# A two-layer transformer block on one core: norm steps ahead of weight splits in the order of work, and an output projection that ends tile by tile

## The chip, the cores and the metric

One core of a Trainium2 chip runs the whole program. The metric is the time of one execution on the device in microseconds (us); the kernel before takes 1361.4 us (median of three runs, 1358.92 to 1363.43). The engines are TensorE (PE, with its weight loads PEld), VectorE (DVE), ScalarE (ACT), GpSimd (POOL) and SyncE (SP), which here only issues DMAs. Each engine carries out its own instructions in their order; engines wait for one another by semaphores.

## What is computed

Two layers act on 256 rows of `ctx` and 256 rows of `x`, each row 1024 wide, all in fp32. Cut to what matters:

```python
for l in range(2):
    with_ctx = l == 0
    sx1, ax1, gx1, sx2, ax2, gx2 = split(silu(c) @ w_ada[l] + b_ada[l], 6)      # likewise for ctx
    hx = rmsnorm(x, g_pre_mix[l]) * (1.0 + ax1) + sx1                           # likewise hc from ctx
    yc, yx = token_mixer(hc, hx, w_in[l], ..., w_out[l])                        # mLSTM, HGRN2, attention, then @ w_out
    x = x + gx1 * rmsnorm(yx, g_post_mix[l])                                    # "post-norm"
    hx = rmsnorm(x, g_pre_ffn[l]) * (1.0 + ax2) + sx2                           # "norm"
    x = x + gx2 * rmsnorm((silu(hx @ w_gate[l]) * (hx @ w_up[l])) @ w_down[l], g_post_ffn[l])
    # with_ctx: the same two updates for ctx
return x
```

## The kernel before

The 512 rows lie in four tiles of 128: tiles 0 and 1 are `ctx` (half 0), tiles 2 and 3 are `x` (half 1). The residual of a tile is `R[t]`. In layer 0 both halves go through everything, half 1 first in the FFN; in layer 1 only half 1 goes on after the mixer.

**Weights.** Each fp32 product is made of reduced-precision products of a high and a low part. `wload` (L279) brings a piece of a weight matrix (512 KB or less) into `wraw` by a DMA on SP (L292; three buffers), rounds it into `whi` on ACT (L295) and forms the rest `wlo` on DVE (L296), with two buffers of each. Activations lie likewise as `hT[0]` (high) and `hT[1]` (low), transposed. Every piece gives matmuls of `hT[0]` and `hT[1]` with `whi`, and of `hT[0]` with `wlo`, all at L300.

**Modulation sums.** `silu(c) @ w_ada` is not made on PE: `ada_group` loads `araw` pieces of 512 KB on SP (L210; two buffers) and DVE adds each, scaled, to `accq` and `acc` (L224, L226). It is a generator that is stepped between other work, for the next layer in particular.

**Norms.** `post_norm` (L443) sums the squares in `zss` on DVE (L446), takes the power on POOL (L448) and updates `R[t]` on DVE (L450); then the norm takes the square of `R[t]` on ACT (L411), `rstd` on POOL (L401, L402) and scales into `nsc` on DVE (L413). `norm_T` transposes `nsc` on PE in four banks of PSUM `pt` (L430), applies the modulation on ACT (L436) and DVE (L438), rounds `hT[0]` on ACT (L440) and forms `hT[1]` on DVE (L441).

**The output projection.** `out_first` does the half of `w_out` that is known early, `out_rest` the other half: four column blocks `cb`, each two PSUM halves of a bank, for both tiles of a half. When two blocks are done, `ev_z` takes the result out: `Z` on DVE (L1151) and its squares on ACT (L1153). After the FFN's down projection `ev_d` does the like in quarters (L1274, L1277, L1278). `late_norm` is the norm of half 1 at the start of layer 1, built when that layer's first matmuls are written.

**What sets the order.** The program is written as straight code, and a scheduler puts each engine's instructions in an order by priority: the place in the code, less an offset where the code asks for one. `wload`'s two splits have an offset of 2000 (`AHEAD`); norms, sums and projections have none. Where two instructions are ready, the one with the smaller number goes first on its engine; the order is fixed when the program is built. Tiles from a pool are handed out in the order of the code, so a step also waits for the tile that it reuses.

## Time and profile before

| | us |
|---|---|
| median of three runs | 1361.4 (1358.92 to 1363.43) |
| the profiled execution | 1362.55 |
| its span, first to last instruction | 1360.8 |
| PE busy | 1294.5 (95% of the span) |
| DVE busy | 897.5 (66%) |
| ACT busy | 619.0 (45%) |
| POOL busy | 198.9 (15%) |
| mean granted clock of PE, share of full | 0.984 |

In the page, busy time is a share of the whole span, and the chain of work that ended last is followed back from the last instruction to what released each step. A timeline gives for each instruction its start, its length, its engine and line, what it writes and reads, a count where several follow on one another, and in brackets how long the engine was idle before it and what ended that. A table of stretches gives for each stretch its length, the busy time and instructions (x) of PE, PEld, DVE, ACT and POOL, then PEclk, the busy share of the DMA engines and the GB/s moved. PEclk is the clock that PE was granted as a share of full: 0.50 is 1.2 GHz, 1.00 is 2.4 GHz.

### The profile page before, as it was taken

What the parts mean: (1) busy time and instruction counts of PE and PEld (TensorE: products, weight loads), DVE (VectorE), ACT (ScalarE), POOL (GpSimd) and SP (SyncE); (2) the same over time, 40 slices, a digit from 0 to 9 for tenths busy, and PEclk for the clock granted to TensorE, in tenths of its full rate; (3) what the DMA queues carried; (4) which work ended last, traced back from release to release, by engine and by line L of the source; (5) the groups of instructions that cost most, each with busy time, mean ns of one, the idle gap of its engine ahead of it and who ended that gap; (6) DMA issues with size and microseconds to landing.
All of it is one profiled execution on the core that took longest, in us unless ns stands there. A gap on an engine that the chain in (4) does not pass through costs nothing.

```text
span 1360.8 us, 25400 instructions
## 1 busy us (share of the span) xinstructions
PE 1294.5 (95%) x10166; PEld 1159.7 (85%) x10166; DVE 897.5 (66%) x1586; ACT 619.0 (45%) x1176; POOL 198.9 (15%) x316
## 2 busy tenths in 40 slices
PE   7998999999989999999999999899999997999997
PEld 5776889788988898998899888778897997999997
DVE  4899989564688997476335348566856555555555
ACT  3436452586255652222322236546526825544443
POOL 3123102111042200001000013133111201000001
PEclk9999999999989899999999999899999999899999
DMA  9872526132244687487335335532331314456663
GB/s 284 239 217 65 174 62 194 36 114 70 94 140 156 196 257 219 140 258 245 96 94 186 93 108 141 142 93 65 101 95 50 121 47 139 124 181 181 184 184 125
DMA packets 171348, 194.20 MB, mean 143 GB/s; under 512 B 10620, under 2 KB 158502, under 8 KB 171230
## 3 DMA queue, kind: packets, MB, share of 16 engines
q1 hardware_dynamic: 169806, 188.89, 45.9%
q0 software_dynamic: 1424, 3.68, 0.9%
q8 instruction: 80, 1.31, 0.4%
q14 instruction: 38, 0.31, 0.1%
HBM read 191.47 MB, written 1.08 MB: 141 GB/s over the span
## 4 chain that ended last, share of the span: by engine, by line
PE 79%; DVE 8%; ACT 5%; POOL 3%; issue 2%; DMA 2%; SPq 0%; DVEq 0%; POOLq 0%; ACTq 0%
PE mm L300 65%; PE mx L1102 2%; DVE wlo L296 2%; PE mx L957 1%; PE mx L979 1%; ACT whi L295 1%; PE mm L1090 1%; POOL rstd L402 1%; PE mx L430 1%; PE mx L973 1%; ACT Dt L1011 1%; DMA wraw<-in_w_ffn_down_dram 1%; PE mx L855 1%; PE ada L231 1%; POOL rstd L401 1%
## 5 line engine op out<-in xcount | busy, mean ns | idle before, releaser
L295 ACT CAST whi<-wraw 128x1024 fp32r<-128x1024 f32 (+1 forms) x254 | 259.0, 1021 | 447.0 <-PE mm L300 388.1
L296 DVE TENSOR_TENSOR wlo<-wraw,whi 128x1024 fp32r<-128x1024 f32 (+1 forms) x250 | 299.5, 1199 | 199.5 <-ACT whi L295 97.0
L300 PE MATMUL mm<-hT,whi 128*128 128x256 f32 (+1 forms) x1920 | 356.9, 337 | 3.6 <-ACT hT L440 2.1
L300 PEld LDWEIGHTS mm<-hT,whi 128*128 128x128 f32 x1920 | 296.9, 192 | 42.5 <-issue 3.3
L300 PE MATMUL mm<-whi,hT 128*128 128x256 f32 (+1 forms) x1792 | 265.7, 294 | 4.5 <-ACT hT L1133 2.2
L300 PEld LDWEIGHTS mm<-whi,hT 128*128 128x128 f32 x1792 | 234.5, 193 | 22.3 <-issue 10.5
L300 PE MATMUL mm<-hT,wlo 128*128 128x256 f32 (+1 forms) x960 | 185.5, 335 | 0.0
L300 PEld LDWEIGHTS mm<-hT,wlo 128*128 128x128 f32 x960 | 150.4, 191 | 17.5 <-issue 0.4
L300 PE MATMUL mm<-wlo,hT 128*128 128x256 f32 (+1 forms) x896 | 138.8, 292 | 0.0
L300 PE MATMUL mm<-whi,GT 128*128 128x256 f32 x1032 | 134.6, 284 | 1.0 <-ACT whi L295 1.0
L300 PEld LDWEIGHTS mm<-whi,GT 128*128 128x128 f32 x1032 | 128.2, 192 | 3.7 <-issue 1.7
L300 PEld LDWEIGHTS mm<-wlo,hT 128*128 128x128 f32 x896 | 119.1, 192 | 8.4 <-issue 7.6
L226 DVE SCALAR_TENSOR_TENSOR accq<-araw,csil,accq 128x1024 f32<-128x1024 f32 x63 | 81.3, 1295 | 25.9 <-DMA araw<-in_w_ada_dram 25.5
L300 PE MATMUL mm<-wlo,GT 128*128 128x256 f32 x516 | 71.3, 283 | 0.7 <-DVE wlo L296 0.7
L300 PEld LDWEIGHTS mm<-wlo,GT 128*128 128x128 f32 x516 | 65.9, 192 | 1.3 <-DVE wlo L296 1.3
L226 DVE SCALAR_TENSOR_TENSOR acc<-araw,csil,acc 128x1024 f32<-128x1024 f32 x49 | 63.7, 1321 | 4.5 <-DMA araw<-in_w_ada_dram 4.4
L401 POOL TENSOR_SCALAR rstd<-hss 128x1 f32<-128x1 f32 (+2 forms) x44 | 17.0, 386 | 242.7 <-ACT hsq L631 159.0
L1278 POOL TENSOR_TENSOR Z<-Z,gg 128x256 f32<-128x256 f32 x18 | 15.8, 889 | 246.7 <-ACT sqz L1277 246.7
L1254 DVE TENSOR_TENSOR sg<-sg,mm 128x256 f32<-128x256 f32 (+1 forms) x48 | 24.7, 518 | 34.2 <-PE mm L300 33.5
L964 ACT ACTIVATE e<-mx,damx 128x512 f32<-128x512 f32 (+1 forms) x48 | 29.3, 617 | 24.9 <-DVE damx L961 24.9
L786 ACT COPY Ck<-Kh 128x512 f32<-128x512 f32 (+1 forms) x56 | 28.8, 524 | 25.7 <-DVE Kh L811 17.9
L957 PE MATMUL mx<-qkT,qkT 48*128 48x512 f32 (+1 forms) x96 | 34.2, 562 | 6.3 <-ACT e L964 5.5
(275 smaller groups left out, 1474.2 us busy)
## 6 DMA issues: line engine op xcount, KB each, us to landing
araw<-in_w_ada_dram SPq DMA_DIRECT2D x80, 512.0 KB
wraw<-in_w_in_dram SPq DMA_DIRECT2D x68, 512.0 KB
wraw<-in_w_ffn_gate_dram SPq DMA_DIRECT2D x48, 512.0 KB
wraw<-in_w_ffn_up_dram SPq DMA_DIRECT2D x48, 512.0 KB
wraw<-in_w_ffn_down_dram SPq DMA_DIRECT2D x44, 512.0 KB
wraw<-in_w_out_dram SPq DMA_DIRECT2D x24, 512.0 KB
aw<-in_w_ada_dram SPq DMA_DIRECT2D x16, 512.0 KB
wraw<-in_w_in_dram SPq DMA_DIRECT2D x12, 256.0 KB
```

What stands on the lines that cost most here:

```text
L226: V.scalar_tensor_tensor(out=a, in0=raw, scalar=csil[:, k, r:r + 1], in1=a, op0=ALU.mult, op1=ALU.add)
L231: PE.matmul(ps[32 * j:32 * j + 32, :], lhsT=esel[:, r, :], rhs=accs[j // 2][r][:, (j % 2) * 512:(j % 2 + 1) * 512], start=r == 0, stop=r = ...
L295: S.copy(hi[:, :nk, :n], raw[:, :nk, :n])
L296: (eng or V).tensor_tensor(lo[:, :nk, :n], raw[:, :nk, :n], hi[:, :nk, :n], op=ALU.subtract)
L300: PE.matmul(ps, lhsT=lhs, rhs=rhs, start=first, stop=last, skip_group_check=True)
L401: G.tensor_scalar(o[:, :width], ss, 1.0 / n, EPS, ALU.mult, ALU.add)
L786: S.copy(C[:, q0:].rearrange("p (a b i) -> p b a i", b=2, i=m), vap(K_, 2 * m * pq0, [[512 + m, 2], [2 * m, np_], [1, m]]))
L957: PE.matmul(ps[:, :nk], lhsT=qkT[0][64 * j:64 * j + DA_D, h, t * P:(t + 1) * P], rhs=qkT[1][64 * j:64 * j + DA_D, h, :nk], start=True, sto ...
L964: S.activation(e[:, j, :nk], pp[j][:, :nk], AF.Exp, bias=mx[:, 2 + j:3 + j], scale=sc, accum_out=mx[:, 4 + j:5 + j])
L1102: PE.matmul(po[:, i, d_, :], lhsT=W[d_, s_][0][:, t * P - W[d_, s_][2]:(t + 1) * P - W[d_, s_][2]], rhs=Vml[:, s_, h, :], start=n_ == 0, s ...
L1254: V.tensor_mul(sg[:, :n], sg[:, :n], ps)
L1278: (V if cb == 3 else G).tensor_tensor(zs, zs, gg[1 if t < 2 else 0][:, cb * 256:(cb + 1) * 256], op=ALU.mult)
```

## The change

It has three parts. `CHAIN = 4000`: the post-norms and norms before the FFN, after the FFN and at the start of layer 1 get an offset of 4000, more than the weight splits' 2000. The output projection of the last half (half 0 in layer 0, half 1 in layer 1) does column blocks 0 and 1 as before; for blocks 2 and 3 it does all that belongs to one tile, takes `Z` out, and does this tile's post-norm right there, inside the offset; then the other tile. So the post-norm of that half no longer stands in the FFN's part. `NAH = 2`: `norm_T` asks for its first two banks at once and writes the transposes of its first tile into both before those of its second.

```diff
--- before.py
+++ after.py
@@ -78,9 +78,11 @@
 
 NMM = 4
 
-HP1, AHEAD = 20, 2000
+HP1, AHEAD, CHAIN = 20, 2000, 4000
 
 WARM = (7, 0, 10, 0, 2, 4, 6, 3)
+
+NAH = 2
 
 KPOOL = (0, 1, 0, 0, 0, 0, 0)
 
@@ -423,11 +425,20 @@
         xn, hs = scr
         if xs is None:
             xs = [norm_rows(2 * hf + i, xn[:, i]) for i in range(2)]
+        pts = [pst([P, 2, 2, P]) for _ in range(NAH)]
+
+        for i in range(2):
+            for kp in range(NAH):
+                for kk in range(2):
+                    PE.transpose(pts[kp][:, kk, i, :], xs[i][:, (2 * kp + kk) * P:(2 * kp + kk + 1) * P], ident)
         for kp in range(KD // 2):
-            pt = pst([P, 2, 2, P])
-            for kk in range(2):
-                for i in range(2):
-                    PE.transpose(pt[:, kk, i, :], xs[i][:, (2 * kp + kk) * P:(2 * kp + kk + 1) * P], ident)
+            if kp < NAH:
+                pt = pts[kp]
+            else:
+                pt = pst([P, 2, 2, P])
+                for kk in range(2):
+                    for i in range(2):
+                        PE.transpose(pt[:, kk, i, :], xs[i][:, (2 * kp + kk) * P:(2 * kp + kk + 1) * P], ident)
             h = hs[:, kp % 2]
             for kk in range(2):
                 k = 2 * kp + kk
@@ -1171,14 +1182,25 @@
             for t in tt_:
                 Z[t] = yp.tile([P, D], F32, tag=f"Y{t}", name=nm("Z"))
                 zss[t] = sm.tile([P, 2], F32, tag=f"zss{t}", name=nm("zss"))
+            ws = {}
             for cb in range(4):
-                hi, lo = wload([w_out[l, 0:512, cb * 256:(cb + 1) * 256]])
+                hi, lo = ws[cb] = wload([w_out[l, 0:512, cb * 256:(cb + 1) * 256]])
+                if hf != halves[-1] or cb < 2:
+                    for t in tt_:
+                        out_mm(t, cb, hi, 0, True, False, False)
+                    for t in tt_:
+                        out_mm(t, cb, lo, 0, False, False, True)
+                        if cb % 2:
+                            ev_z(t, cb // 2)
+            if hf == halves[-1]:
+
                 for t in tt_:
-                    out_mm(t, cb, hi, 0, True, False, False)
-                for t in tt_:
-                    out_mm(t, cb, lo, 0, False, False, True)
-                    if cb % 2:
-                        ev_z(t, cb // 2)
+                    for i in range(2):
+                        for cb in (2, 3):
+                            out_mm(t, cb, ws[cb][i], 0, i == 0, False, i == 1)
+                    with tc.high_priority(offset=CHAIN):
+                        ev_z(t, 1)
+                        post_norm(t, Z[t], zss[t])
 
         ada_flush()
         if full:
@@ -1222,9 +1244,11 @@
             u1, s1_ = mod_cols(l, 1)
             for hf in halves:
                 scr = norm_scr(ff, "nsc")
-                for t in (2 * hf, 2 * hf + 1):
-                    post_norm(t, Z[t], zss[t])
-                norm_T(u1, s1_, hf, scr)
+                with tc.high_priority(offset=CHAIN):
+                    if hf != halves[-1]:
+                        for t in (2 * hf, 2 * hf + 1):
+                            post_norm(t, Z[t], zss[t])
+                    norm_T(u1, s1_, hf, scr)
             Z = {t: yp.tile([P, D], F32, tag=f"Y{t}", name=nm("Z")) for t in qt}
             zss = {t: sm.tile([P, 4], F32, tag=f"zss{t}", name=nm("zss")) for t in qt}
             groups = [(0, 8), (8, 8), (16, 6)]
@@ -1291,14 +1315,18 @@
                         gemm_bt([(d_src(cb), h_) for cb, h_ in zip(held, holds)], gact, tt_,
                                 lambda ci, t, ps: ev_d([t], ps, held[ci]))
                     if last:
-                        for t in tt_:
-                            post_norm(t, Z[t], zss[t], out if l == DEPTH - 1 else None)
-                        if l + 1 < DEPTH and tt_[0] == 0:
-                            norm_T(u0, s0, 0, norm_scr(ff, "nsc"))
-                        elif l + 1 < DEPTH:
-                            scr = norm_scr(stg, "qk")
-                            xs = [norm_rows(t, scr[0][:, t - 2]) for t in tt_]
-                            late_norm = lambda u=u0, s=s0, scr=scr, xs=xs: norm_T(u, s, 1, scr, xs)
+                        with tc.high_priority(offset=CHAIN):
+                            for t in tt_:
+                                post_norm(t, Z[t], zss[t], out if l == DEPTH - 1 else None)
+                            if l + 1 < DEPTH and tt_[0] == 0:
+                                norm_T(u0, s0, 0, norm_scr(ff, "nsc"))
+                            elif l + 1 < DEPTH:
+                                scr = norm_scr(stg, "qk")
+                                xs = [norm_rows(t, scr[0][:, t - 2]) for t in tt_]
+
+                                def late_norm(u=u0, s=s0, scr=scr, xs=xs):
+                                    with tc.high_priority(offset=CHAIN):
+                                        norm_T(u, s, 1, scr, xs)
         gst.close()
```


**DVE in layer 0, at the end of the output projection of half 0.** Before, these rows stand among its matmuls (`R_4253` and `R_4255` are the residuals of tiles 2 and 3, half 1; L1134 belongs to the mixer's output):

```order
L450 SCALAR_TENSOR_TENSOR R_4253<-Z_4883,rstd_5310,R_4253 128x1024
L296 TENSOR_TENSOR wlo_5204<-wraw_5202,whi_5203 128x1024
L450 SCALAR_TENSOR_TENSOR R_4255<-Z_4885,rstd_5315,R_4255 128x1024
L1134 SCALAR_TENSOR_TENSOR hT_143<-mx_5150,gcol_4245,hT_142 128x256
L1134 SCALAR_TENSOR_TENSOR hT_143<-mx_5159,gcol_4245,hT_142 128x256
L413 TENSOR_SCALAR nsc_5307<-R_4253,rstd_5320 128x1024
L413 TENSOR_SCALAR nsc_5307<-R_4255,rstd_5326 128x1024
```

With the change, from the last `Z` of half 0 on (L1162 is `ev_z`, L457 and L461 `post_norm`, L415 the norm, L298 `wlo`; `R_4249` and `R_4251` are tiles 0 and 1):

```order
L1162 TENSOR_TENSOR Z_5170<-mm_5022,gg_4311 128x512
L461 SCALAR_TENSOR_TENSOR R_4249<-Z_5168,rstd_5279,R_4249 128x1024
L457 TENSOR_SCALAR zss_5171,ss_5309<-zss_5171 128x2
L457 TENSOR_SCALAR zss_4884,ss_5318<-zss_4884 128x2
L457 TENSOR_SCALAR zss_4886,ss_5323<-zss_4886 128x2
L298 TENSOR_TENSOR wlo_5439<-wraw_5437,whi_5438 128x1024
L461 SCALAR_TENSOR_TENSOR R_4251<-Z_5170,rstd_5311,R_4251 128x1024
L461 SCALAR_TENSOR_TENSOR R_4253<-Z_4883,rstd_5320,R_4253 128x1024
L461 SCALAR_TENSOR_TENSOR R_4255<-Z_4885,rstd_5325,R_4255 128x1024
L298 TENSOR_TENSOR wlo_5479<-wraw_5477,whi_5478 128x1024
L415 TENSOR_SCALAR nsc_5317<-R_4253,rstd_5330 128x1024
L415 TENSOR_SCALAR nsc_5317<-R_4255,rstd_5336 128x1024
```

The four rows of tiles 2 and 3 stood ahead of the last `Z` of half 0 and stand behind it now, behind the post-norm of tiles 0 and 1.

**SP at the same place**, the loads of gate and up weights and of `araw` for the modulation sums. Before:

```order
L292 DMA wraw_5437<-in_w_ffn_gate_dram 128x4x256
L210 DMA araw_5866<-in_w_ada_dram 128x1024
L205 DMA ba_5817<-in_b_ada_dram 2x512
L292 DMA wraw_5477<-in_w_ffn_gate_dram 128x4x256
L205 DMA ba_5817<-in_b_ada_dram 2x512
L292 DMA wraw_5517<-in_w_ffn_up_dram 128x4x256
L205 DMA ba_5817<-in_b_ada_dram 2x512 x2
L292 DMA wraw_5551<-in_w_ffn_up_dram 128x4x256
L210 DMA araw_5900<-in_w_ada_dram 128x1024
L292 DMA wraw_5595<-in_w_ffn_gate_dram 128x4x256
L238 DMA gp_6971<-in_g_post_mix_dram 2x512 x2
L210 DMA araw_5942<-in_w_ada_dram 128x1024
```

With the change:

```order
L212 DMA araw_5866<-in_w_ada_dram 128x1024
L294 DMA wraw_5437<-in_w_ffn_gate_dram 128x4x256
L212 DMA araw_5900<-in_w_ada_dram 128x1024
L212 DMA araw_5942<-in_w_ada_dram 128x1024
L294 DMA wraw_5477<-in_w_ffn_gate_dram 128x4x256
L207 DMA ba_5817<-in_b_ada_dram 2x512
L294 DMA wraw_5517<-in_w_ffn_up_dram 128x4x256
L207 DMA ba_5817<-in_b_ada_dram 2x512 x3
L212 DMA araw_5976<-in_w_ada_dram 128x1024
L240 DMA gp_6971<-in_g_post_mix_dram 2x512 x2
L294 DMA wraw_5551<-in_w_ffn_up_dram 128x4x256
```

Three `araw` loads stand ahead of the second gate piece where there was one.

**DVE at the start of layer 1**, the norm of half 1 (`nsc_8928`; L665 adds biases to the layer's first results). Before:

```order
L413 TENSOR_SCALAR nsc_8928<-R_4253,rstd_8931 128x1024
L413 TENSOR_SCALAR nsc_8928<-R_4255,rstd_8937 128x1024
L665 TENSOR_TENSOR Vda_8948<-mm_8961,brow_9031 128x128
L665 TENSOR_TENSOR gt_8951<-mm_8961,brow_9031 128x16
L665 TENSOR_TENSOR Vhg_8960<-mm_8961,brow_9031 128x256
L296 TENSOR_TENSOR wlo_9095<-wraw_9093,whi_9094 128x2x400
L665 TENSOR_TENSOR Vda_8948<-mm_8962,brow_9031 128x128
L665 TENSOR_TENSOR gt_8951<-mm_8962,brow_9031 128x16
L665 TENSOR_TENSOR Vhg_8960<-mm_8962,brow_9031 128x256
L296 TENSOR_TENSOR wlo_9115<-wraw_9113,whi_9114 128x2x400
L438 TENSOR_SCALAR nsc_8928<-mx_9055,u_8398,adaC_6491 128x256
L438 TENSOR_SCALAR nsc_8928<-mx_9064,u_8398,adaC_6491 128x256
```

With the change (L415 is `nsc`, L449 applies the modulation):

```order
L415 TENSOR_SCALAR nsc_8928<-R_4253,rstd_8931 128x1024
L298 TENSOR_TENSOR wlo_9025<-wraw_9023,whi_9024 128x2x400
L415 TENSOR_SCALAR nsc_8928<-R_4255,rstd_8937 128x1024
L298 TENSOR_TENSOR wlo_9095<-wraw_9093,whi_9094 128x2x400
L449 TENSOR_SCALAR nsc_8928<-mx_9055,u_8398,adaC_6491 128x256
```

The modulation step stood behind six bias additions and two `wlo` and now stands behind one `wlo` after the last `nsc`.

## Rows read from the trace of the kernel before

**Rows 1.** The page: the chain of work that ended last, by engine

```profile
PE 79%; DVE 8%; ACT 5%; POOL 3%; issue 2%; DMA 2%; SPq 0%; DVEq 0%; POOLq 0%; ACTq 0%
```

**Rows 2.** Table of stretches: two in which PE has no pause

```profile
474.00:815.00 341.00, 341.00 (x2059) 302.22 (x2058) 194.67 (x229) 99.49 (x131) 11.21 (x14) 1.00 0.54 170
864.00:900.00 36.00, 36.00 (x184) 32.18 (x183) 14.67 (x22) 19.64 (x26) 9.89 (x14) 0.96 0.42 117
```

**Rows 3.** PE's timeline at seam A

```profile
452.80 1.47 PE L430 MATMUL mx<-ident,nsc 128*128 128x128 f32 x12
454.03 1.19 PE L300 MATMUL mm<-hT,whi 128*128 128x256 f32 x8
457.35 0.80 PE L300 MATMUL mm<-hT,whi 128*128 128x256 f32 x2 [2.12 <-ACT hT L440]
458.86 1.65 PE L300 MATMUL mm<-hT,whi 128*128 128x256 f32 x6 [0.72 <-DVE hT L441]
```

**Rows 4.** Table of stretches: the half clock at seam A

```profile
458.00:464.00 6.00, 5.28 (x25) 5.14 (x25) 4.75 (x7) 2.13 (x3) 0.61 (x1) 0.50 0.64 206
```

**Rows 5.** DVE's timeline at seam A

```profile
434.91 1.28 DVE L450 SCALAR_TENSOR_TENSOR R<-Z,rstd,R 128x1024 f32<-128x1024 f32 x1
436.10 1.22 DVE L296 TENSOR_TENSOR wlo<-wraw,whi 128x1024 fp32r<-128x1024 f32 x1
...
440.70 0.75 DVE L413 TENSOR_SCALAR nsc<-R,rstd 128x1024 f32<-128x1024 f32 x1 [0.72 <-POOL rstd L402]
...
449.95 1.27 DVE L226 SCALAR_TENSOR_TENSOR acc<-araw,csil,acc 128x1024 f32<-128x1024 f32 x1
...
454.61 1.27 DVE L1151 TENSOR_TENSOR Z<-mm,gg 128x512 f32<-128x512 f32 x2
455.81 0.98 DVE L438 TENSOR_SCALAR nsc<-mx,u,adaC 128x256 f32<-128x256 f32 x2
...
458.13 1.28 DVE L441 TENSOR_TENSOR hT<-nsc,hT 128x512 fp32r<-128x512 f32 x2
```

**Rows 6.** POOL's timeline at seam A

```profile
431.79 1.95 POOL L448 TENSOR_TENSOR rstd<-ss,mhalf 128x1 f32<-128x1 f32 x2
...
437.45 1.11 POOL L401 TENSOR_SCALAR rstd<-ss 128x1 f32<-128x1 f32 x1 [3.05 <-ACT nsc L411]
...
439.79 0.25 POOL L401 TENSOR_SCALAR rstd<-ss 128x1 f32<-128x1 f32 x1 [0.59 <-ACT nsc L411]
```

**Rows 7.** PE's waits from 400 to 480 us: in total, times, longest

```profile
PE mx L1128 <- DVE Y L638: 1.4, 1, 1.4
```

**Rows 8.** Chain of waits, in order of time: a load of araw, issue to landing

```profile
85.27 4.02 DMA araw<-in_w_ada_dram
```

**Rows 9.** PE's timeline at seam B

```profile
831.50 0.55 PE L430 MATMUL mx<-ident,nsc 128*128 128x128 f32 x3 [1.32 <-DVE nsc L413]
...
834.90 1.20 PE L430 MATMUL mx<-ident,nsc 128*128 128x128 f32 x9 [1.05 <-DVE nsc L413]
...
844.49 1.72 PE L300 MATMUL mm<-whi,hT 128*128 128x400 f32 x8
...
856.58 2.61 PE L430 MATMUL mx<-ident,nsc 128*128 128x128 f32 x11 [1.08 <-DVE nsc L413]
...
862.05 3.02 PE L300 MATMUL mm<-whi,hT 128*128 128x400 f32 x8
```

**Rows 10.** DVE's timeline at seam B

```profile
855.77 0.75 DVE L413 TENSOR_SCALAR nsc<-R,rstd 128x1024 f32<-128x1024 f32 x1 [0.72 <-POOL rstd L402]
...
859.72 0.99 DVE L296 TENSOR_TENSOR wlo<-wraw,whi 128x800 fp32r<-128x800 f32 x1 [1.07 <-ACT whi L295]
860.62 0.99 DVE L438 TENSOR_SCALAR nsc<-mx,u,adaC 128x256 f32<-128x256 f32 x2
```

**Rows 11.** PE's timeline at seam C

```profile
1156.92 0.87 PE L430 MATMUL mx<-ident,nsc 128*128 128x128 f32 x3 [7.87 <-DVE nsc L413]
```

**Rows 12.** DVE's timeline at the end

```profile
1355.26 0.43 DVE L1278 TENSOR_TENSOR Z<-Z,gg 128x256 f32<-128x256 f32 x1 [0.64 <-ACT sqz L1277]
```

## The prediction

> **What bounds the kernel now.** I read first the page's chain of work that ended last: TensorE (PE) makes 79% of it, VectorE (DVE) 8%, ScalarE (ACT) 5% and GpSimd (POOL) 3% [rows 1]. Next came the table of stretches. From 474 to 815 us PE is busy all the time at full clock [rows 2]. Nothing that this change moves can help there, and nothing that is lost ahead of such a stretch can be won back inside it. So the time is decided at the seams, where a normed activation has to come through DVE, ACT and POOL before PE can go on. There are four: **A**, layer 0's output projection into its FFN (430 to 474 us); **B**, layer 0's FFN into layer 1 (824 to 867 us); **C**, layer 1's output projection into its FFN (1149 to 1164 us); **D**, the end. Then I read the timelines of PE and DVE at each, and the order of the instructions there, which tells what is moved; all durations are from the trace.
>
> The number of operations hardly changes: the same norms, splits, sums and matmuls are issued, and the transposes ahead are the same sixteen transposes in another order. So no term comes from added or removed work; each is a wait that grows or shrinks.
>
> **A: the loss.** Before, the post-norm and norm of half 1 (tiles 2 and 3) are done by 441 us, while PE still works on half 0's output projection: the R updates stand at 434.91 us and after, the last nsc at 440.70 us [rows 5]. PE has no wait up to the twelve transposes of 452.80 us, at the projection's end, does these and eight gate matmuls, and then waits 2.12 us for hT, until 457.35 us, and 0.72 more [rows 3]. In the changed order the post-norm of half 0, now written inside the projection and carrying the same lead of 4000, comes first on DVE, and half 1's zss, R and nsc stand behind it. They can't start before half 0's last matmul has ended, and no gate matmul can start before them, because the gate blocks begin with half 1.
>
> The end of the projection comes a little earlier. PE's wait of 1.4 us for Y [rows 7] stands behind a head norm on POOL that itself stands behind two post-norm steps of 1.95 us [rows 6]; these are moved away, so I put the last matmul at 452.8 - 1.4 = 451.4 us.
>
> From there DVE has, in its new order, up to the first hT1 of half 1: one Z (1.27 / 2 = 0.64), four R (4 x 1.28 = 5.12), two wlo (2 x 1.22 = 2.44), two nsc (2 x 0.75 = 1.50), three modulation sums acc or accq (3 x 1.27 = 3.81), a pair of L438 (0.98) and the first of an L441 pair (1.28 / 2 = 0.64) [rows 5], 15.1 us, and some 0.4 for three zss. Back to back these overlap by 0.09 (434.91 + 1.28 against 436.10), 14 times, so 1.3 less; the last nsc waits 0.72 for its rstd, as the row of 440.70 does. Together 14.9, so hT1 is there at about 466.3 us, where before PE could go on at 458.86 [rows 3]: 7.4 us later. By then PE had 8 + 2 gate matmuls behind it; now it has two, since PE takes its instructions in order and the third needs hT1. Eight matmuls at the half clock seen there, 1.65 / 6 = 0.28 each [rows 3], add 2.2, at full clock (1.19 for the eight) 1.2. The clock is half now at that point, and I take 2.1. **A costs 9.5 us.** Lower bound 7.5: the eight matmuls and the 0.72 hidden. Upper bound 12: one modulation sum more on the path (1.27) and the half clock of 458 to 464 us [rows 4], which the idle time before it brought on, going on for longer.
>
> Each POOL step in that chain is also a possible delay: the step of 437.45 us took 1.11 beside an R on DVE, the same step at 439.79 us 0.25 [rows 6]. I count it inside the upper bound. The Trainium skill, on the page "SBUF — State Buffer" (section "SBUF: two separate sides"), says that a GpSimd instruction and a VectorE instruction with two SBUF inputs exclude each other for their whole length; the row agrees, and by that rule alone A would be 1 to 2 us dearer than my 9.5.
>
> In the same stretch the araw loads move ahead of gate and up weights in the queue of SyncE (SP). A load takes about 4.02 us to land [rows 8]. By the order, each is issued at least 4 us before its sum is due, and the later weights are due when PE is already 9.5 us late, so I price this at nothing; without that cover it is the second rival.
>
> **B: the gain.** Down projection of layer 0: PE waits 1.32 and 1.05 us for nsc [rows 9]. In the new order nsc comes ahead of the wlo that delays it by up to 1.2 us, and its square on ACT ahead of a cast; I leave 0.7 of the 2.37, so 1.7 won. At the layer's start the late norm of half 1 has nsc at 855.77, then bias additions, two wlo and a wait of 1.07 before L438 at 860.62 [rows 10]: 4.85 us. Now one wlo (0.99) stands between, 0.75 + 0.99 = 1.7; as the transposes and the bias step on POOL must also be done, I count 2.9 won. The matmuls that follow run at half clock, eight in 3.02 us against 1.72 for the same eight earlier [rows 9]; with less idle time ahead I count 0.8 of that 1.3 and the like of the next four. **B gives 5.4 us**, 3 if the casts that are pushed back stall PE in turn, 7.5 if nothing takes the place of the waits. The earlier start carries on, since PE has no pause from 864 to 900 us [rows 2].
>
> **C.** PE waits 7.87 us, then does three transposes [rows 11]. Tile 2 is finished earlier, since the last matmuls of tile 3 no longer stand between its own, and its R with it, but the chain of tile 3 still runs after the last matmul, and a wlo of some 1.2 us now stands in it. At best one R (1.28) and most of the three transposes (0.87) leave the path, 2 us; at worst nothing. **I take 1.0.**
>
> **D.** The last zss comes ahead of a Z of 0.43 us [rows 12]: **0.3 won**.
>
> **The sum**: + 9.5 - 5.4 - 1.0 - 0.3 = + 2.8 us. It is made against the profiled execution, 1362.55 us (span 1360.8), so 1365.3 there. That execution stands 1.15 above the median of the three runs shown, 1361.4, inside their spread, so the forecast for the median is 1361.4 + 2.8 = about 1364 us. A measurement of this kernel can tell about 0.3% (4.1 us) from no change; the forecast is inside that.
>
> **Rivals.**
> 1. *A costs next to nothing* (about 1, as when half 1's norms still run under the projection on the chip): 1 - 5.4 - 1.3 = - 5.7, 1356 us. For it: the change gives these steps the highest rank. Against it: instructions of one engine run in their order, and in that order they stand behind Z of half 0's last tile. 0.13.
> 2. *DVE waits for an araw load in A.* Three sums stand in the chain of tiles 2 and 3; if a load is issued late, because SP waits for a weight buffer ahead of it, DVE stops at the sum and every norm step behind it stops too. It decides from the point where a load is issued less than 4.02 us [rows 8] ahead of its sum, and costs up to that once: + 2.8 + 4.0 = + 6.8, 1368 us. For it: the norm steps can't pass a sum on DVE's queue. Against it: the buffers are freed earlier than before. 0.20.
> 3. *POOL's steps wait for DVE in A*, twice 0.86 (1.11 against 0.25 [rows 6]): + 4.5, 1366 us. The Trainium skill's page named above would have it so. 0.08.
> 4. *The clock doesn't fall at B.* It falls after 856 us, when PE has waited three times in a row; with the shorter waits it may stay at 2.4 GHz, and the eleven transposes of 2.61 us and the matmuls behind them would be done in about half the time: 2 to 3 us more, so 1361 us. The Trainium skill ("TensorE: Matmul & The Clock Gate", Part 1) says that throttled is the default and activity lifts it; by that rule it hangs on how much idle time is left there. 0.12.
>
> **How the numbers follow.** The forecast has 0.47, with its own range of 1359 to 1368: 0.32 of it within 0.3%, 0.14 slower, 0.01 faster. Rival 1 is faster (0.13), rival 2 slower (0.20), rival 3 slower (0.06) or the same (0.02), rival 4 the same (0.12). So faster 0.14, same 0.46, slower 0.40. The bounds of the terms, 7.5 - 7.5 - 2 - 0.4 and 12 - 3, give - 2.4 to + 9, so 1359 to 1370.5; to take in part of rival 1 and the spread of the runs I widen to 1357 to 1371.
>
> **What would show it.** In the changed profile PE should have long waits (over 10 us in all) between about 451 and 467 us, with half 1's R after the last Z of half 0, and the stretch of unbroken matmuls should begin some 9 us later. At B the two waits for nsc should be under 0.6 each and layer 1's second matmul group should start about 4.6 us sooner, measured from the FFN's end. At C PE's wait should be within 7 to 8 us. The prediction is wrong if PE's wait at A is short, if DVE shows waits for araw there, or if at B a wait for whi or wlo replaces those for nsc.

## The result, and the profile after

The changed kernel takes 1367.5 us (median of seven runs, 1365.43 to 1369.45) against 1360.45 for the kernel before in the runs timed with it (seven, 1358.92 to 1363.43): a ratio of 1.0053 [1.0043, 1.0064], or 7.1 us slower. The forecast was 2.8 us slower, 1364.0, with a range of 1357 to 1371. So sign and range held, and the size was short by 4.3 us.

One caution comes first. The two profiled executions differ by only 3.1 us (1365.69 against 1362.55), since before's lies 2.1 above its median and after's 1.9 below. What a seam costs is therefore read from two executions of each kernel where that is possible, and from medians of kernels that have only a part of the change.

The page of after, busy time and the chain of work that ended last:

```profile
PE 1291.2 (95%) x10166; PEld 1155.2 (85%) x10166; DVE 894.7 (66%) x1586; ACT 618.8 (45%) x1176; POOL 212.0 (16%) x316
...
PE 74%; DVE 8%; ACT 5%; issue 5%; POOL 4%; DMA 3%; SPq 1%; DVEq 0%; POOLq 0%; ACTq 0%
```

Against [rows 1] PE's share of the chain is 74% instead of 79%, POOL's 4% instead of 3%. POOL's busy time is 13 us more than before's 198.9, with the same operations. Now seam A. PE's timeline of after:

```profile
450.43 1.12 PE L302 MATMUL mm<-wlo,hT 128*128 128x256 f32 x8
463.17 1.12 PE L433 MATMUL mx<-ident,nsc 128*128 128x128 f32 x4 [11.62 <-DVE nsc L415]
464.64 1.12 PE L433 MATMUL mx<-ident,nsc 128*128 128x128 f32 x4 [0.35 <-DVE nsc L415]
...
467.48 1.12 PE L441 MATMUL mx<-ident,nsc 128*128 128x128 f32 x4 [0.88 <-DVE nsc L449]
468.25 0.78 PE L302 MATMUL mm<-hT,whi 128*128 128x256 f32 x2
469.73 3.33 PE L302 MATMUL mm<-hT,whi 128*128 128x256 f32 x14 [0.70 <-DVE hT L452]
```

The projection ends at 450.43 + 1.12 = 451.55 us (forecast: 451.4). Then PE stands still for 11.62 us, until the first `nsc` of half 1, where before had, behind the projection, only [rows 3]'s 2.12 and 0.72. DVE's timeline shows what stood ahead of that `nsc`:

```profile
441.30 1.26 DVE L228 SCALAR_TENSOR_TENSOR accq<-araw,csil,accq 128x1024 f32<-128x1024 f32 x1
442.50 1.27 DVE L228 SCALAR_TENSOR_TENSOR acc<-araw,csil,acc 128x1024 f32<-128x1024 f32 x1
443.69 1.21 DVE L298 TENSOR_TENSOR wlo<-wraw,whi 128x1024 fp32r<-128x1024 f32 x1
444.83 1.27 DVE L228 SCALAR_TENSOR_TENSOR accq<-araw,csil,accq 128x1024 f32<-128x1024 f32 x1
...
451.79 0.68 DVE L1162 TENSOR_TENSOR Z<-mm,gg 128x512 f32<-128x512 f32 x1
453.71 1.29 DVE L461 SCALAR_TENSOR_TENSOR R<-Z,rstd,R 128x1024 f32<-128x1024 f32 x1 [1.24 <-POOL rstd L459]
...
456.83 3.68 DVE L461 SCALAR_TENSOR_TENSOR R<-Z,rstd,R 128x1024 f32<-128x1024 f32 x3 [0.47 <-POOL rstd L459]
460.43 1.22 DVE L298 TENSOR_TENSOR wlo<-wraw,whi 128x1024 fp32r<-128x1024 f32 x1
462.36 0.75 DVE L415 TENSOR_SCALAR nsc<-R,rstd 128x1024 f32<-128x1024 f32 x1 [0.72 <-POOL rstd L404]
463.83 0.75 DVE L415 TENSOR_SCALAR nsc<-R,rstd 128x1024 f32<-128x1024 f32 x1 [0.72 <-POOL rstd L404]
...
468.99 1.29 DVE L452 TENSOR_TENSOR hT<-nsc,hT 128x512 fp32r<-128x512 f32 x2
```

All four R updates come after the last `Z` (451.79), where half 1's two stood at 434.91 and after in [rows 5]. DVE waits four times for POOL: 1.24 + 0.47 + 0.72 + 0.72 = 3.15 us. What held POOL is in its timeline:

```profile
440.87 0.20 POOL L1130 TENSOR_SCALAR gcol<-cols 128x3 f32<-128x3 f32 x1 [7.07 <-DVE hT L1145]
441.04 5.12 POOL L1131 TENSOR_SCALAR gcol<-cols 128x2 f32<-128x2 f32 x1
446.10 0.09 POOL L1132 MEMSET gcol<- 128x3 f32 x1
446.16 2.22 POOL L241 TENSOR_TENSOR gp<-gp,ba 64x512 f32<-64x512 f32 x1
...
453.08 0.59 POOL L459 TENSOR_TENSOR rstd<-ss,mhalf 128x1 f32<-128x1 f32 x1
...
455.16 1.64 POOL L459 TENSOR_TENSOR rstd<-ss,mhalf 128x1 f32<-128x1 f32 x1 [0.95 <-DVE zss L457]
```

Seam B, PE's timeline of after: the waits that answer to [rows 9].

```profile
842.04 0.66 PE L433 MATMUL mx<-ident,nsc 128*128 128x128 f32 x4 [1.26 <-DVE nsc L415]
...
863.71 0.63 PE L433 MATMUL mx<-ident,nsc 128*128 128x128 f32 x4 [0.56 <-DVE nsc L415]
...
865.87 0.66 PE L433 MATMUL mx<-ident,nsc 128*128 128x128 f32 x4 [0.51 <-DVE nsc L415]
...
868.88 0.62 PE L302 MATMUL mm<-whi,hT 128*128 128x400 f32 x2 [0.31 <-ACT hT L451]
869.99 1.36 PE L302 MATMUL mm<-whi,hT 128*128 128x400 f32 x6 [0.49 <-DVE hT L452]
```

And seam C, where [rows 11] had 7.87:

```profile
1161.57 1.08 PE L433 MATMUL mx<-ident,nsc 128*128 128x128 f32 x4 [7.10 <-DVE nsc L415]
```

To put the time in its place, the table takes the same PE instruction ahead of and behind each seam (before's start in the column's head, from PE's timelines) and tells how much later (+) it starts than in before's profiled execution. What a seam cost or gave is the difference of the two columns around it; the kernels are described below.

| kernel | ahead of A, 415.91 | behind A, 508.24 | ahead of B, 802.80 | behind B, 872.94 | ahead of C, 1134.97 | behind C, 1208.84 |
|---|---|---|---|---|---|---|
| after | +0.34 | +12.05 | +12.05 | +5.45 | +5.43 | +3.34 |
| after, again | +1.92 | +12.77 | +12.77 | +6.49 | +8.04 | +5.97 |
| before, again | +0.18 | -0.64 | -0.64 | -2.54 | -1.00 | -1.83 |
| layer 0 as before | -0.71 | +2.49 | +2.49 | -3.26 | -0.18 | -1.73 |
| FFN end only | 0.00 | +0.21 | +0.21 | -6.23 | -3.14 | -3.99 |
| half 0 first | -0.60 | +11.54 | +11.54 | +5.27 | +6.71 | +4.81 |
| own buffers | +1.73 | +9.15 | +8.58 | +2.08 | +3.48 | +2.17 |
| sums held | -11.85 | +6.76 | +11.81 | +5.28 | +8.27 | +6.67 |
| late transposes | +0.48 | +6.47 | +6.47 | -0.09 | -0.18 | -2.26 |
| projection's hT first | +0.10 | +0.96 | +0.96 | -4.80 | -2.64 | -4.52 |
| layer 0, no offset | +0.27 | +3.02 | +3.02 | -2.21 | -2.23 | -4.29 |
| the same, no transposes ahead | -0.78 | +2.51 | +2.51 | -3.25 | -0.21 | -1.57 |
| transposes ahead alone | -1.23 | -1.03 | -1.03 | -5.19 | -3.85 | -5.20 |

So between the first executions A costs 12.05 - 0.34 = 11.7 us, B gives 6.6 back and C 2.1, and from A to B nothing moves, as [rows 2] would have it. Two stretches outside the seams differ as well, also between executions of the same kernel. Ahead of A it is up to 2 us (after's second execution had a granted clock of 0.50 from 271 to 277 us, its first 0.72, both of before 1.00). Between B and C, in layer 1's mixer, before's second execution loses 1.5 us against its first, after's two 0 and 1.5, others up to 3.1.

### The profile page after: what moved, and what is told of

It is laid out like the page before. It is cut to its first block, busy times and chain, and to the rows that moved or that the text cites. A ratio compares the mean times of both kernels' runs of the same rounds, so it can differ in the third digit from the quotient of the medians.

```text
span 1364.0 us, 25395 instructions
## 1 busy us (share of the span) xinstructions
PE 1291.2 (95%) x10166; PEld 1155.2 (85%) x10166; DVE 894.7 (66%) x1586; ACT 618.8 (45%) x1176; POOL 212.0 (16%) x316
## 4 chain that ended last, share of the span: by engine, by line
PE 74%; DVE 8%; ACT 5%; issue 5%; POOL 4%; DMA 3%; SPq 1%; DVEq 0%; POOLq 0%; ACTq 0%
PE mm L302 62%; DVE wlo L298 2%; PE mx L1113 2%; PE mx L968 1%; POOL rstd L404 1%; POOL rstd L403 1%; PE mx L990 1%; ACT whi L297 1%; PE mm L1101 1%; PE mx L984 1%; PE mx L866 1%; PE ada L233 1%; PE mm L164 1%; ACT Dt L1022 1%; DVE R L461 1%
## 5 line engine op out<-in xcount | busy, mean ns | idle before, releaser
L298 DVE TENSOR_TENSOR wlo<-wraw,whi 128x1024 fp32r<-128x1024 f32 (+1 forms) x250 | 300.7, 1204 | 201.2 <-PE mm L302 90.6
L404 POOL TENSOR_TENSOR rstd<-rstd,mhalf 128x1 f32<-128x1 f32 (+2 forms) x58 | 40.2, 694 | 4.8
```

The costliest lines, as they stand in the source:

```text
L298: (eng or V).tensor_tensor(lo[:, :nk, :n], raw[:, :nk, :n], hi[:, :nk, :n], op=ALU.subtract)
L404: G.tensor_tensor(o[:, :width], o[:, :width], mhalf[:, :width], op=ALU.pow)
```

## The experiments

**How steady a profile is.** Before and after were profiled once more each.

> The kernel before, unaltered, for a second profile. Read from single profiles, the four seams sum to + 3.3 us, while the medians differ by 7.1, and the stretches at half clock differ from profile to profile. If each seam's own cost is stable, this profile has PE waits at A, B and C within 0.3 us of the first, and differs from it only in how long the clock stays at half behind the same waits (3.4 or 1.7 us worth of work each time, or none); its span then lies between 1357 and 1362 us. If a seam's waits themselves differ by over 1 us, the readings by seam can't be trusted.

> The changed kernel, unaltered, for a second profile. If the seams are stable: PE's wait at A 11 to 12 us again, some 11 to 13 us lost there against either profile of the kernel before, waits at B as in the first; and, since the first execution was 1.9 us under the median, one more stretch of half clock somewhere in the mixer of layer 1 or at a seam. Span 1364 to 1367 us.

Measured: 1360.22 and 1368.38 us. Between the two second executions A costs 10.85 + 0.82 = 11.7 us, the same as between the first, though not every wait is (after's for `nsc` at A is 10.7 us instead of 11.6, before's for the modulation step at B 2.56 instead of 2.12). C gives 1.2 us instead of 2.1, and B 6.28 - 1.90 = 4.4 instead of 6.6, because before's own B is 1.9 us shorter this time. The tables of stretches show with what: at the place where before had a granted clock of 0.50 (857 to 866 us, nine us at layer 1's first transposes), the second execution of before has 0.84; after has 1.00 both times. First before's second execution, then after's first, then after's second:

```profile
854.00:863.00 9.00, 5.36 (x25) 4.32 (x26) 7.60 (x16) 4.67 (x9) 0.52 (x1) 0.84 0.56 147
```

```profile
863.00:872.00 9.00, 7.13 (x42) 6.07 (x42) 7.73 (x14) 5.57 (x10) 1.77 (x3) 1.00 0.78 208
```

```profile
864.00:873.00 9.00, 7.14 (x43) 6.02 (x42) 7.83 (x14) 5.52 (x10) 1.89 (x3) 1.00 0.80 205
```

**The parts.** First layer 0's projection and post-norms are written as before, inside the offset; everything else is as in after.

```diff
-                if hf != halves[-1] or cb < 2:
+                if hf != halves[-1] or cb < 2 or full:
...
-            if hf == halves[-1]:
+            if hf == halves[-1] and not full:
...
-                    if hf != halves[-1]:
+                    if hf != halves[-1] or full:
                         for t in (2 * hf, 2 * hf + 1):
```

> The change, with the output projection of layer 0 written as in the kernel before (no tile-by-tile end, the post-norm of half 0 in the FFN's part); the offset of 4000 stays on its norms, and layer 1 and the FFN ends stay changed. Theory Q: half 1's norm is under the projection again, the same as with buffers of its own, 1350 to 1356 us. Rival P: here the loss goes too, but not with buffers of its own, so this run is some 10 us faster than that one. Rival S: 1361 to 1365.

Measured: 1359.32 us, 0.999 [0.998, 1.0001], slower than all of Q's range; A costs 3.2 instead of 11.7. By medians that part of the change alone is 1.0053 - 0.999 = 0.0063, some 8.6 us of loss.

Then the other way round: before, with only the offset on the norms at the FFN's end and on `late_norm` (B and D, without the transposes ahead).

```diff
                     if last:
-                        for t in tt_:
+                        with tc.high_priority(offset=CHAIN):
+                            for t in tt_:
...
+                                def late_norm(u=u0, s=s0, scr=scr, xs=xs):
+                                    with tc.high_priority(offset=CHAIN):
+                                        norm_T(u, s, 1, scr, xs)
```

> The kernel before, with the offset of 4000 only on the norms after the FFN and on the late norm of layer 1 (seams B and D); the output projections and the transposes as before. The profiles give B + D as 6.6 + 0.4 us: 1353 to 1355 us if these gains come from the offset alone; 1356 to 1358 if part of B comes from the transposes of one tile ahead, which this kernel lacks; no gain, 1360, if B's gain was only the later arrival at that seam (weights loaded further ahead after the loss at A).

Measured: 1357.21 us, 0.9975 [0.9966, 0.9984], so B and D give 3.4 us by the median. The profile has 6.4 at B, but 3.1 of them are lost again in layer 1's mixer, at a granted clock of 0.57:

```profile
1042.00:1050.00 8.00, 7.52 (x30) 6.02 (x31) 3.09 (x10) 4.00 (x13) 0.58 (x2) 0.57 0.01 2
```

So the time lies in the range on record for a B that lacks the transposes ahead, but not for that reason. All else in the change (A, C, the transposes ahead) is then worth 1.0053 - 0.9975 = 0.0078, some 10.6 us.

**Tile by tile, or the place of the post-norm?** Layer 0's matmuls and `ev_z` go in the old order; only half 0's post-norm stays written inside the projection, ahead of half 1's.

```diff
-                if hf != halves[-1] or cb < 2:
+                if hf != halves[-1] or cb < 2 or full:
...
-                            out_mm(t, cb, ws[cb][i], 0, i == 0, False, i == 1)
+                            if not full:
+                                out_mm(t, cb, ws[cb][i], 0, i == 0, False, i == 1)
                     with tc.high_priority(offset=CHAIN):
-                        ev_z(t, 1)
+                        if not full:
+                            ev_z(t, 1)
                         post_norm(t, Z[t], zss[t])
```

> The change, with the output projection of layer 0 doing its matmuls in the order of the kernel before; only the place of half 0's post-norm in the code stays changed: right behind that projection, ahead of half 1's post-norm, with the offset. By the order of instructions half 1's R and nsc stand behind half 0's last Z again. Theory Q: this place alone brings the loss at A, 10 to 13 us, and PE's wait for nsc is over 10 us there: 1364 to 1369 us. Rival P (the tile-by-tile matmuls are the loss; undoing them took 9.6 us off A): A + 2 to + 4, 1357 to 1360.

Measured: 1365.84 us, 1.0035 [1.0022, 1.0047]; A costs 12.1, with the same wait in PE's timeline:

```profile
462.21 1.12 PE L433 MATMUL mx<-ident,nsc 128*128 128x128 f32 x4 [11.23 <-DVE nsc L415]
```

So it is the place of the post-norm in the code (Q on record), not the tile-by-tile end (P), that costs the time at A. By medians 0.0018 (2.4 us) is left between this kernel and after; the intervals overlap, and what that is isn't shown.

**Why the place decides.** Both halves have the same offset, and half 1's data is ready first, so the scheduler could still have taken half 1's steps. But `post_norm` takes its small tiles `ss` and `rstd` from buffers that all tiles share by a tag, and these are handed out in the order of the code. Here half 0's post-norm gets buffers of its own:

```diff
-    def post_norm(t, Z, zss, out=None):
+    def post_norm(t, Z, zss, out=None, tg=""):
-        s1 = sm.tile([P, 1], F32, tag="ss", name=nm("ss"), bufs=4)
+        s1 = sm.tile([P, 1], F32, tag="ss" + tg, name=nm("ss"), bufs=2 if tg else 4)
...
-                        post_norm(t, Z[t], zss[t])
+                        post_norm(t, Z[t], zss[t], tg="o")
```

> The change, with one thing altered: the post-norm that stands inside the output projection takes its two small results (ss, rstd) from buffers of its own, two of each, in place of the ones that all norms share. By the order of instructions half 1's zss, R and nsc then stand on DVE ahead of half 0's last Z again, as in the kernel before; no priority is altered. Theory Q (queue: half 1's norm loses its cover only because it must take its buffers after half 0's post-norm): the loss at A, 12.1 us by the profiles, goes, and B, C and D stay, so 1352 to 1356 us, and down to 1350 if the transposes ahead also shorten A below its length in the kernel before. Rival P (projection: the tile-by-tile end itself delays A, because it needs both last weight pieces at once): the loss stays, 1364 to 1368. Rival S (sums: the modulation sums that now fill DVE are the loss): two thirds of it stay, 1361 to 1365.

Measured: 1362.99 us, 1.0017 [1.0005, 1.0029]. Half 1's R updates stand early again and the wait of 11 us is gone; by the medians 1.0053 - 1.0017 = 0.0036, some 4.9 us, come back. But Q's forecast is missed, and the time lies in rival S's range: A still costs 7.4 in the profile, for PE has other waits:

```profile
445.89 0.69 PE L433 MATMUL mx<-ident,nsc 128*128 128x128 f32 x2 [4.49 <-DVE nsc L415]
448.48 1.56 PE L433 MATMUL mx<-ident,nsc 128*128 128x128 f32 x6 [1.91 <-DVE nsc L415]
...
471.85 0.65 PE L433 MATMUL mx<-ident,nsc 128*128 128x128 f32 x4 [1.60 <-DVE nsc L415]
...
477.65 0.65 PE L433 MATMUL mx<-ident,nsc 128*128 128x128 f32 x4 [2.65 <-DVE nsc L415]
```

Half 1's transposes have the offset too, so they now stand in PE's queue ahead of the projection's matmuls. These could hardly have run, though: three of the four steps that bring their input `hT` (L1145) stand on DVE behind both `nsc`. DVE's timeline, then POOL's:

```profile
435.24 2.48 DVE L461 SCALAR_TENSOR_TENSOR R<-Z,rstd,R 128x1024 f32<-128x1024 f32 x2 [0.72 <-POOL rstd L459]
...
448.35 0.86 DVE L1145 SCALAR_TENSOR_TENSOR hT<-mx,gcol,hT 128x256 fp32r<-128x256 f32 x2
```

```profile
441.25 2.89 POOL L241 TENSOR_TENSOR gp<-gp,ba 64x512 f32<-64x512 f32 x1 [4.16 <-DVE ba L235]
444.22 0.19 POOL L403 TENSOR_SCALAR rstd<-ss 128x1 f32<-128x1 f32 x1
```

And `nsc` is late because on POOL its `rstd` stands behind `gp`, a step of the modulation that first waits 4.16 us for DVE. In before `gp` came behind both of half 1's `rstd` steps of [rows 6], at 442.92 us. "Layer 0 as before" shows the same 4.49, 1.91 and 4.16. No run moved `gp` alone, so what it costs isn't shown.

**What the modulation sums add.** In after's code the sums get a factor that is a copy of `csil` made behind half 1's last `hT[1]`; so they can't stand in the chain.

```diff
+                if full and hf == halves[0]:
+                    csil_now[0] = const.tile([P, KD, 2], F32, tag="csil2", name="csil2")
+                    V.scalar_tensor_tensor(out=csil_now[0], in0=hT[1][:, :, 256:258], scalar=0.0, in1=csil[:, :, 0:2],
+                                           op0=ALU.mult, op1=ALU.add)
```

> The change, with the modulation sums of the next group held back: they take their scale from a copy of it that is written after half 1's last hT1, so none of them can stand in the chain of half 1. Nothing else of the chain is altered. Theory Q: of the chain only the three sums ahead of hT1 and the one ahead of half 0's zss go, 3.6 to 4.8 us, so 1362 to 1364 us, and PE still waits over 7 us for nsc at A. Rival S: 1356 to 1359, and PE's wait for nsc at A falls under 4 us. A cost of its own may come from the sums being later, up to 2 us at the end of the FFN.

Measured: 1367.07 us, 1.0045 [1.0028, 1.0061], slower than both ranges on record. Behind A this kernel is 5.3 us ahead of after, but not all of that is the chain: the sums have also left the stretch ahead of A, and the projection ends at 438.50 + 1.12 = 439.62 us.

```profile
438.50 1.12 PE L304 MATMUL mm<-wlo,hT 128*128 128x256 f32 x8
449.37 1.11 PE L435 MATMUL mx<-ident,nsc 128*128 128x128 f32 x4 [9.75 <-DVE nsc L417]
...
454.15 1.93 PE L304 MATMUL mm<-hT,whi 128*128 128x256 f32 x14 [0.20 <-DVE hT L454]
```

From there to the first gate matmul that needs `hT[1]` it is 454.15 - 439.62 = 14.5 us, in after 469.73 - 451.55 = 18.2. So 3.7 us are sums in the chain, and PE still waits 9.75 for `nsc`, both as Q had it. The gain is lost again before B (+6.76 becomes +11.81), since the sums have to be done all the same. PE's two largest waits from 480 to 620 us, in total, times and longest:

```profile
PE ada L235 <- DVE accq L230: 3.2, 2, 1.9
PE mm L304 <- DVE sg L1284: 3.0, 2, 2.0
```

So holding the sums back wins nothing.

**Who waits behind what is raised.** If PE's early transposes are the trouble in "layer 0 as before", holding them back should bring A to nothing. Half 0's norm gets no offset, and half 1's transposes use an identity matrix that DVE writes only after `Z` of column blocks 0 and 1.

```diff
+                if full and hf == halves[-1] and cb == 1:
+                    V.scalar_tensor_tensor(out=id2[0], in0=Z[tt_[0]][:, 0:P], scalar=0.0, in1=ident, op0=ALU.mult, op1=ALU.add)
...
-                with tc.high_priority(offset=CHAIN):
+                with tc.high_priority(offset=0 if full and hf == halves[-1] else CHAIN):
...
-                    norm_T(u1, s1_, hf, scr)
+                    norm_T(u1, s1_, hf, scr, idn=id2[0] if full and hf != halves[-1] else None)
```

> As the run with layer 0 written as before and the offset kept (1359.3 us), with one alteration for half 1: its transposes take an identity matrix that DVE writes behind the first Z of half 0's projection, so that on PE they stand behind two thirds of that projection instead of ahead of it; and half 0's norm has no offset. Theory W (in-order wait: with early norms it is only the transposes, put into PE's queue before nsc is there, that stall PE at A, 7.7 us in that run): PE's wait for nsc at A falls under 1 us, the waits of the kernel before for hT (2.1 + 0.7) go too, so A gains 2 to 5 us against the kernel before and the time is 1349 to 1353 us. Rival: early norms cost by crowding DVE and POOL, so that the projection's wlo and Z come late; then 1356 to 1360, with waits for wlo or whi at A.

Measured: 1361.14 us, 1.0009 [1.0000, 1.0018]: A costs 6.0, more than with the early transposes (3.2). PE has one wait of 7.48, for the projection's own input:

```profile
447.62 2.78 PE L302 MATMUL mm<-whi,hT 128*128 128x256 f32 x10 [7.48 <-DVE hT L1146]
```

and DVE's timeline shows why that `hT` was late: it stood behind both `nsc`, and these behind POOL, where `gp` stands ahead of `rstd` as in "own buffers".

```profile
443.82 0.75 DVE L415 TENSOR_SCALAR nsc<-R,rstd 128x1024 f32<-128x1024 f32 x1 [2.06 <-POOL rstd L404]
446.19 0.99 DVE L415 TENSOR_SCALAR nsc<-R,rstd 128x1024 f32<-128x1024 f32 x1 [1.61 <-POOL rstd L404]
447.10 0.86 DVE L1146 SCALAR_TENSOR_TENSOR hT<-mx,gcol,hT 128x256 fp32r<-128x256 f32 x2
```

So holding the transposes back doesn't end the wait (W on record falls). It arises in DVE's queue, where what is raised makes what stands behind it wait (V). Next, with this edit kept, the projection's input is raised above the norms:

```diff
-            y_T(halves[-1], (0, 1))
+            with tc.high_priority(offset=6000 if full else 0):
+                y_T(halves[-1], (0, 1))
```

> The run with late transposes (1361.1 us), with an offset of 6000 on the step that brings the mixer's output into hT for half 0's projection. There, PE's one long wait at A, 7.5 us, was for that hT, which stood on DVE behind both nsc of half 1, and these waited 2.1 and 1.6 us for POOL. Now three of the four rows of hT stand ahead of the first nsc, one behind it. Theory V (each engine's in-order queue: whatever the raised steps wait for, the steps behind them wait too): that wait falls to 2 to 4 us, A from + 6.5 to + 1 to + 3.5, so 1356 to 1359. If the wait stays over 6 us, it wasn't DVE's queue.

Measured: 1357.71 us, 0.9978 [0.9969, 0.9988]. The waits for `hT` are 1.23 and 2.15 instead of 7.48, and A costs 0.9:

```profile
441.75 1.30 PE L302 MATMUL mm<-whi,hT 128*128 128x256 f32 x4 [1.23 <-DVE hT L1146]
445.20 0.79 PE L302 MATMUL mm<-whi,hT 128*128 128x256 f32 x2 [2.15 <-DVE hT L1146]
```

**A block with no offset.** "Layer 0 as before", with `offset=0 if full else CHAIN`; then the same without the transposes ahead (`NAH = 0`). Both were meant to leave A as it was.

> The change, with layer 0 up to its FFN as in the kernel before: no tile-by-tile end, the post-norm of half 0 in the FFN's part, and no offset on the norms there (the transposes of one tile ahead stay). Seams B, C and D as changed. If the loss at A comes from these edits alone, A is 0 within 1 us, B gives 6.5 and C 2 in the profile, so some 1352 to 1355 us by the median, 2 to 4 us faster than with the FFN end alone (1357.2). If it is 1357 or more, C gives nothing, or the transposes ahead cost at A what they give elsewhere.

> The change with all that concerns layer 0 up to its FFN undone (as in the kernel before) and without the transposes ahead (NAH = 0); the offset of 4000 after the FFN, at layer 1's start and end, and layer 1's projection that ends tile by tile stay. From the profiles so far: A 0, B - 5 to - 6.5, C - 2, D - 0.3. Against the FFN end alone (1357.2, which has B and D) C should show as 1 to 2 us: 1355 to 1356.5. If it is 1357 or more, C gives nothing in the median. If it is above 1359, the transposes ahead are needed for B or C.

Measured: 1359.29 us, 0.9992 [0.9983, 1.0001], and 1358.57 us, 0.9981 [0.9973, 0.9990]. A isn't as before in either (+2.8 and +3.3): with an offset of 0 a pair of R updates still stands ahead of half 1's `hT[1]` on DVE, and PE waits for that where [rows 3] has 0.72; from the second kernel:

```profile
460.70 1.65 PE L302 MATMUL mm<-hT,whi 128*128 128x256 f32 x6 [3.38 <-DVE hT L452]
```

The transposes ahead aren't the reason, since the second kernel lacks them. The order of layer 0 without any block was not run together with the rest. The second kernel has C changed and is no faster than "FFN end only", so the medians don't show C's gain; its A masks up to 3.3.

**The transposes ahead alone.** Before, with `NAH = 2` and its new loop in `norm_T`, nothing else.

> The kernel before with the transposes of one tile ahead (NAH = 2) alone. The run with layer 0 written as before but these transposes had A at + 3.0, its R of half 0 ahead of half 1's hT1 on DVE. If the transposes ahead do that alone: A + 2.5 to + 3.5, the rest within 1 us, so 1361.5 to 1364. If A needs the edits elsewhere in the order: 1359.5 to 1360.5, like the kernel before.

Measured: 1358.57 us, 0.9982 [0.9971, 0.9993]: 2.5 us faster, where none was expected; its profile has 4.2 at B and nothing at A (0.2 lost).

## Why the prediction was right or wrong

- **A, the mechanism: right.** Half 1's steps stand behind half 0's on DVE, PE stands still from the projection's end, and the loss stays through the FFN. "Half 0 first" and "own buffers" show the reason that the prediction read from the order without naming it: the tiles shared by tag. Rival 1 fell with that. That the projection ends at 451.55 (451.4 foreseen) is partly luck: PE's wait for Y shrank from 1.41 to 0.47 us and didn't go, but a wait of 0.78 for half 1's `nsc` (at 441.51 us, where the prediction saw no wait) and four of its transposes left this stretch too.
- **A, the size: 9.5 foreseen, 11.7 measured.** The step that was mis-sized is "the last nsc waits 0.72 for its rstd": it counted one wait of DVE for POOL, and there were four, 3.15 us. PE went on at 469.73, 3.4 us after the 466.3 foreseen. Of these 2.4 are the waits for POOL, 0.4 is that `Z` began at 451.79 and not 451.4, and the rest goes with the overlaps, of which the sum took off fourteen (1.3 us) and a step that waits has none. Taken back are 0.9, since the eight matmuls and the half clock behind them cost 1.2 (the 12.05 less 469.73 - 458.86) instead of 2.1, and the 0.3 that lie ahead of A. The lower bound of 7.5 doesn't follow from its own terms, which give 7.4 - 0.7 = 6.7; the upper bound of 12 held.
- **Why POOL came late.** Ahead of the first wait, 1.24, stand the step of 441.04 that took 5.12 us, `gp`, two DMA issues and the wait for their landing; at the second, 0.47, a power took 1.64 us. In "half 0 first", with the same 5.12, DVE has a `wlo` ahead of the last `Z` in place of the first wait, and A is as long; so what the 5.12 is worth isn't shown. It is the place that rival 3 named, at more than its price of 1.7. Rival 2 did not happen: no wait for `araw` stands in this chain.
- **B: the mechanism right, the size within the profiles, the median below it.** It foresaw 5.4, and the profiles give 6.6 and 4.4; the median of "FFN end only" gives 3.4 with D in it, against 5.7 for the two terms. Two steps of the term did not hold. The half clock, counted at 0.8, is not there each time: before's profile happened to have 0.50, and its second execution 0.84. And "the earlier start carries on" was shown only up to 900 us: in layer 1's mixer "FFN end only" loses 3.1 us again, before's second execution 1.5. That the change brings this about isn't shown. Rival 4 came true in that after's clock stays at 1.00, but it was priced against one execution of before. Of the waits in the forecast, those of the layer's start went down (0.56 and 0.51), of the two in the down projection one is gone and the other, at 842.04 us, still has 1.26 against a promised 0.6.
- **C: as foreseen in the profiles, not resolved by medians.** Its wait is 7.10, inside the 7 to 8 foreseen, and the pairs give 2.1 and 1.2 (foreseen 1.0). Every profile with C changed gains 1.3 to 2.1 us there against before's first; those without it 0 to 0.9, and "transposes ahead alone" 1.35. **D** was not tried by itself. **The transposes ahead** were priced at nothing by themselves, and are worth 2.5 us alone.
- **The sum.** By medians A, C and the transposes ahead come to + 10.6 (foreseen: 9.5 - 1.0 = 8.5), B and D to - 3.4 (foreseen - 5.7). The first misses by 2.1, the second by 2.3; the split takes it that the parts add up.

Four versions beat both kernels, "FFN end only" (0.9975), "projection's hT first" (0.9978), "layer 0, no offset" without the transposes ahead (0.9981) and "transposes ahead alone" (0.9982); their intervals overlap, so none is shown to be the best.

## What to carry to other kernels

On engines that work in order, raising a chain makes everything behind it wait whenever the chain itself waits (here a projection's input, 7.48 us): ask of each raised step what it waits for, and whether what it passes could have run. Tiles that chains share by a tag tie these chains together in the order of the code, so moving a step in the code moves a queue; give the moved chain buffers of its own. When two profiles are compared, take a seam's cost from an instruction just ahead of it, not from the start. And before a wait or a slow clock is counted as a gain, look at a second execution.

## What the runs showed of the hardware that was not expected

**A POOL step of 5.12 us.** The step of L1131 on 128x2 elements takes 0.20 us in before, and 5.12 in both executions of after and in "half 0 first". Each time DVE had four instructions with two SBUF inputs back to back beside it (441.30 to 446.10 above; POOL's step ends at 441.04 + 5.12 = 446.16). In "own buffers" and "layer 0 as before" it takes 1.22 and 1.23, about the length of one such instruction. That agrees with POOL being kept out for the whole run of them; why it came in when a fifth followed at 446.02 isn't shown. The Trainium skill ("SBUF — State Buffer", section "SBUF: two separate sides") has the one of such a pair that starts first keep the other out for its whole instruction; here POOL's step lasted through four.

**The clock falls in one execution and not in the next.** At B the same kernel, before, had 0.50 and 0.84 over nine us. In the mixer of layer 1 "FFN end only" had 0.57 from 1042 to 1050 us, after's second execution 0.57 from 1056 to 1060, and before's first 1.00 from 1046 to 1054. That alone makes seams read from one pair of profiles uncertain by some 2 us.
